# Encoder trunk on one core: the next weight unit split ahead of the sums of one unit, h a step behind its modulation, another order at the beginning

## The chip, the core and the metric

The kernel runs on one core of a Trainium2 chip. The metric is the device time of one execution in microseconds (us). Matrix products run on TensorE (PE, with its weight loads as PEld), elementwise work on VectorE (DVE) and ScalarE (ACT), a few powers on GpSimd (POOL); SyncE (SP) issues the transfers (DMA) from main memory. Each engine works through its own queue in the order in which the program was laid out, and waits at semaphores for what another engine or a transfer has to deliver first.

## What is computed

Two layers (DEPTH 2) over 256 tokens of width 2048, all in float32. What matters here:

```python
c_act = jax.nn.silu(c)
for l in range(DEPTH):
    mod = c_act @ ada_w[l] + ada_b[l]
    sh_a, sc_a, gt_a, sh_m, sc_m, gt_m = [t[:, None, :] for t in jnp.split(mod, 6, axis=-1)]
    h = rmsnorm(x, norm_mix[l]) * (1.0 + sc_a) + sh_a
    qa, ka, va, qb, kb, vb, ga, gb = split_cols(h @ w_in[l])
    ...
    merged = jax.nn.sigmoid(ga) * ya + jax.nn.sigmoid(gb) * yb
    x = x + gt_a * (merged @ w_out[l])
    h = rmsnorm(x, norm_ffn[l]) * (1.0 + sc_m) + sh_m
    u = depthwise_conv(h @ w_up[l], conv_w[l], conv_b[l])
    g, v = jnp.split(u, 2, axis=-1)
    x = x + gt_m * ((jax.nn.silu(g) * v) @ w_down[l])
```

`ya` and `yb` are two kinds of attention over the projected q, k and v. So before the first projection can be complete, x has to be normalised and modulated by `sc_a` and `sh_a`, and these come from a product of silu(c) with a 2048 x 12288 matrix per layer.

## The kernel before

**Weights.** All six weight matrices of a layer are cut into blocks of 128x128 and laid out in the order in which they are used (`block_stream`, L85). Sixteen blocks are a unit of 1 MB. `unit` (L274) fetches one with a transfer on SP into a buffer `raw` (four buffers, shared with the matrix for the modulation), and cuts it into two halves of 8 blocks. Each half is split into a rounded high part, by a cast on ACT (L288), and the rest, by a subtraction on DVE (L289), and both go into a tile `hl` (four buffers, so two units). A product is then three matmuls: high by high, high by low, low by high (L297 to L299 where weights are stationary, L355 to L357 where tokens are). `Stream.next_block` (L318) makes a unit when its first block is wanted, or takes one that was made ahead by `prefetch`.

**Modulation.** `ada` (L203) makes one column block of the modulation at a time: a transfer of 1 MB (aw) and one multiply-and-sum on DVE (L220, called a sum here). 96 per layer. The first 32 of layer 0, in the order shift and scale of chunk 0, of chunk 1, and so on, are needed for h. `normed` (L421) makes one chunk of h (16 chunks of 128 features) from two sums, x and the root mean square: a product on DVE (ht, L427), the high part on ACT (h, L430), the low part on DVE (L431). `ada_and_h` (L616) is the job that runs both: a sum, a sum with its chunk of h, in two steps for each chunk.

**Order at the beginning of layer 0.** There are not yet 16 chunks of h when PE could start, so the input projection is cut along its 2048 input features into three parts, with the ends in `K_ENDS` (L40): 9 groups of 512 columns for q, k and v (`tokens`, L345) and then 16 column blocks for the first gate (`features`, L329), first with the chunks that come early, then with more, then with all; sums of the parts are kept in `packA`, `packB` and `ya` (copied on ACT in the first part, L790 and L827, added on DVE later, L792 and L822). The units of these parts are 0 to 12, 13 to 34 and 35 to 51. Each time a unit's blocks are used up, `Stream.tick` (L314) moves the background jobs by their rates (`Paced`, L234): here `ada_and_h` at `FIRST_RATE` steps per unit; `have_h` (L771) runs that job as far as a group needs. The attention's square roots, transposes (`qk_rows`, L500: norm in one tick, turn in the next) and heads are such jobs too. Afterwards a fixed plan per unit (`ADA_PLAN_0`) sets how many sums there are.

**Before the first matmul.** `cact` holds silu(c), spread over 128 rows by four matmuls and silu on ACT (L168 to L171); squares of x are made in turn on ACT and DVE (L632 to L639), summed over chunks on DVE and over partitions by PE; a power on POOL gives the root. Short matmuls (`warm`, L366) run in between.

The order of the instructions of each engine is laid out when the program is built, by a scheduler that starts from the order of the code; the lists below are what came out of it.

Of the kernel before, what the change touches and what calls it, by code (L numbers as in the profile page):

```python
# [15 lines left out]
P = 128  # L16
# [24 lines left out]
    [([2, 2, 2, 3, 3, 4, 4, 4, 4], 6), ([8, 8, 9, 10, 10, 11, 10, 10, 12], 13), ([KC] * 9, KC)],  # L41
# [20 lines left out]
FIRST_RATE = [1.1, 0.85, 0.7]  # L62
# [67 lines left out]
def encoder(ctx: ExitStack, tc: tile.TileContext, a: dict, out: bass.AP):  # L130
# [37 lines left out]
    for i in range(0, D, 512):  # L168
        cb = ax.tile([P, 512], F32, name="cb", tag="ax")
        nc.tensor.matmul(cb[:], one[:], cact[:1, i : i + 512], start=True, stop=True)  # L170
        nc.scalar.activation(out=cact[:, i : i + 512], in_=cb[:], func=AF.Silu)  # L171
    x = const.tile([P, KC, S], F32, name="x")
    skip(64, const)
# [100 lines left out]
    def unit(l, u):  # L274

        raw = rawp.tile([P, UB * P], F32, name=f"w{l}_{u}", tag="raw")
        nc.sync.dma_start(raw[:], a["ws"][l, u])
        halves = []  # L280
        streamed = any(m == "w_in" and mo < GATE_A // P for m, _, mo in STREAMS[l][u * UB : (u + 1) * UB])
        at = OFF if streamed else 0
        for j in range(2):
            n = UB * P // 2
# [3 lines left out]
            nc.scalar.copy(hl[:, 0], r)  # L288
            nc.vector.tensor_tensor(out=hl[:, 1], in0=r, in1=hl[:, 0].bitcast(F32), op=ALU.subtract)  # L289
# [336 lines left out]
    for i in range(0, KC, 4):  # L626
        nc.sync.dma_start(x[:, i : i + 4], a["xT"][:, i : i + 4])

    mean_sq = sm.tile([P, 2], F32, name="ms_in", tag="nsa")
    with tc.high_priority():  # L630
        acc = place("y0", 4, F32, "sq_in")
        for i in range(0, KC, 4):  # L632
            sq = acc if i == 0 else place(f"y{1 + i // 4 % 2}", 4, F32, f"sq_in{i}")
            if i // 4 % 2:
                nc.vector.tensor_tensor(out=sq[:], in0=x[:, i : i + 4], in1=x[:, i : i + 4], op=ALU.mult)
            else:
                nc.scalar.activation(out=sq[:], in_=x[:, i : i + 4], func=AF.Square)
            if i:
                nc.vector.tensor_tensor(out=acc[:], in0=acc[:], in1=sq[:], op=ALU.add)  # L639
# [35 lines left out]
    for l in range(L):  # L675
        st = Stream(l) if l == 0 else nxt
        mod = mods.get(l)
        if l == 0:
            h = led("h0_0")
            job0 = ada_and_h(first_h(h))  # L680
            while done[0] < 2:
                next(job0)
            st.prefetch(1)
            while done[0] < 2 * K_ENDS[0][0][0][0]:
                next(job0)
            mod = mods[0]
# [84 lines left out]
        def have_h(part):  # L771

            while l == 0 and done[0] < 2 * part.stop:
                next(job0)

        for pi, (groups, gates) in enumerate(parts):
# [3 lines left out]
            for g, part in enumerate(groups):  # L780
# [16 lines left out]
                def have(g=g):  # L797
# [255 lines left out]
```

## Time and profile before

| | us |
|---|---|
| median of 3 runs | 2702.55 (2701.57 to 2703.78) |
| the profiled execution | 2700.72 |
| its span, first to last instruction | 2698.9 |
| PE busy | 2665.7 (99%) |
| PEld busy | 2565.9 (95%) |
| DVE busy | 2089.7 (77%) |
| ACT busy | 1405.0 (52%) |

The views used are the waits (engine, line, what it waited for: us in total, times, the longest), the timeline (start, duration, engine, line, operation, tiles, and in brackets the idle time before it and what ended it), groups of instructions by form (busy time, mean ns of one, idle time before and its cause) and stretches (from:to, length, busy time and instructions of PE, PEld, DVE, ACT and POOL, or of one line alone, then the granted clock, the share of the transfer engines and GB/s). A matmul's bar overlaps the next one, so the pace of PE is read from starts, not from durations. Busy shares over the whole span hide that the beginning is different from the rest: the share of PEld by fortieths of the span begins with 5, 8, 7, 9 tenths.

### The profile page before, as it was taken

Reading aid. Unit: us, or ns where it says so; the run is one execution under the profiler, and the core shown is the slowest. Engines: PE = TensorE matmul, PEld = TensorE weight load, DVE = VectorE, ACT = ScalarE, POOL = GpSimd, SP = SyncE. Lnnn points to the kernel's source line nnn. Section 1 sums busy time; section 2 is a strip of 40 time slices with the busy share of each in tenths; the row PEclk is TensorE's granted clock in tenths of the full one; section 3 lists DMA queues with packets and bytes.
Section 4 is the critical chain, followed back from the end, with each engine's and each line's share of the span. In section 5 each row is a group of like instructions: output and inputs, shape, how many; then the busy total and the mean of one; then the engine's idle time right before and its main releaser. Section 6 shows DMA issues by size and latency. Waiting matters only on the chain.

```text
span 2698.9 us, 50255 instructions
## 1 busy us (share of the span) xinstructions
PE 2665.7 (99%) x21128; PEld 2565.9 (95%) x21128; DVE 2089.7 (77%) x2909; ACT 1405.0 (52%) x2078; POOL 32.6 (1%) x24
## 2 busy tenths in 40 slices
PE   8999999999999999999999999999999999999999
PEld 5879799999999999999998889999999999999999
DVE  8897888897987888788886666658878866655664
ACT  4434685445753455355564556555565445543553
POOL 0000100000000000000000000000000000000000
PEclk9999999999999999999999999999999999999999
DMA  8986678987677788788756656667847775555554
GB/s 348 351 337 242 228 271 327 354 302 265 235 298 292 284 303 285 291 298 289 297 210 255 240 203 239 226 245 253 295 176 283 296 259 193 189 202 188 191 199 141
DMA packets 101892, 700.38 MB, mean 260 GB/s; under 512 B 12705, under 2 KB 15009, under 8 KB 17697
## 3 DMA queue, kind: packets, MB, share of 16 engines
q1 hardware_dynamic: 101666, 697.17, 69.9%
q8 instruction: 165, 2.70, 0.4%
q14 instruction: 61, 0.50, 0.1%
HBM read 695.03 MB, written 2.10 MB: 258 GB/s over the span
## 4 chain that ended last, share of the span: by engine, by line
PE 86%; DVE 8%; ACT 2%; DMA 2%; issue 2%; POOL 1%; SPq 0%; DVEq 0%; ACTq 0%; POOLq 0%
PE ps L297 25%; PE ps L299 25%; PE ps L298 25%; PE ps_t L356 3%; PE ps_t L357 3%; PE ps_t L355 3%; DVE hl L289 3%; DVE aw L220 2%; DMA aw<-in_aw 1%; ACT hl L288 1%; PE po L583 1%; PE sc L552 1%; POOL qrs L402 1%; PE tp L577 0%; DVE qn L516 0%
## 5 line engine op out<-in xcount | busy, mean ns | idle before, releaser
L289 DVE TENSOR_TENSOR hl<-w,hl 128x1024 fp32r<-128x1024 f32 x928 | 1130.0, 1222 | 376.0 <-ACT hl L288 374.8
L288 ACT CAST hl<-w 128x1024 fp32r<-128x1024 f32 x928 | 969.6, 1049 | 732.8 <-PE ps L299 493.9
L297 PE MATMUL ps<-h,hl 128*128 128x256 f32 x3328 | 923.6, 278 | 3.1 <-ACT hl L288 3.1
L299 PE MATMUL ps<-h,hl 128*128 128x256 f32 x3328 | 919.5, 277 | 1.3 <-DVE hl L289 1.3
L298 PE MATMUL ps<-h,hl 128*128 128x256 f32 x3328 | 920.6, 277 | 0.0
L297 PEld LDWEIGHTS ps<-h,hl 128*128 128x128 f32 x3328 | 625.6, 188 | 4.5 <-ACT hl L288 4.1
L299 PEld LDWEIGHTS ps<-h,hl 128*128 128x128 f32 x3328 | 624.8, 188 | 1.8 <-DVE hl L289 1.7
L298 PEld LDWEIGHTS ps<-h,hl 128*128 128x128 f32 x3328 | 625.5, 188 | 0.3
L220 DVE CUSTOM_DVE_ANT_0 aw<-aw,cact,ab 128x2048 f32<-128x2048 f32 x189 | 443.6, 2348 | 55.1 <-DMA aw<-in_aw 54.4
L355 PE MATMUL ps_t<-hl,h 128*128 128x512 f32 x576 | 226.0, 399 | 9.2 <-ACT h L430 4.6
L356 PE MATMUL ps_t<-hl,h 128*128 128x512 f32 x576 | 228.2, 396 | 3.8 <-DVE hl L289 3.3
L357 PE MATMUL ps_t<-hl,h 128*128 128x512 f32 x576 | 226.6, 394 | 0.0
L898 DVE SCALAR_TENSOR_TENSOR u<-ps,cw,u 128x255 f32<-128x255 f32 x304 | 146.2, 481 | 65.4 <-ACT u L896 61.1
L896 ACT ACTIVATE u<-ps,cw 128x256 f32<-128x256 f32 x152 | 85.6, 563 | 182.8 <-PE ps L299 182.6
L299 PE MATMUL ps<-merged,hl 128*128 128x256 f32 x512 | 141.6, 277 | 0.8 <-DVE hl L289 0.8
L298 PE MATMUL ps<-merged,hl 128*128 128x256 f32 x512 | 141.5, 276 | 0.0
L297 PE MATMUL ps<-merged,hl 128*128 128x256 f32 x512 | 141.5, 277 | 0.0
L298 PE MATMUL ps<-act_o,hl 128*128 128x256 f32 x512 | 141.4, 276 | 0.0
L299 PE MATMUL ps<-act_o,hl 128*128 128x256 f32 x512 | 141.3, 276 | 0.0
L297 PE MATMUL ps<-act_o,hl 128*128 128x256 f32 x512 | 141.2, 276 | 0.0
L355 PEld LDWEIGHTS ps_t<-hl,h 128*128 128x128 f32 x576 | 108.6, 189 | 34.2 <-ACT hl L288 6.9
L356 PEld LDWEIGHTS ps_t<-hl,h 128*128 128x128 f32 x576 | 109.2, 190 | 30.9 <-DVE hl L289 8.4
(213 smaller groups left out, 4562.2 us busy)
## 6 DMA issues: line engine op xcount, KB each, us to landing
w<-in_ws SPq DMA_DIRECT2D x464, 1024.0 KB, 4.9
aw<-in_aw SPq DMA_DIRECT2D x189, 1024.0 KB, 6.1
bias<-in_bias SPq DMA_DIRECT2D x16, 256.0 KB, 4.8
x<-in_xT SPq DMA_DIRECT2D x4, 512.0 KB, 5.4
aw_o<-in_aw SPq DMA_DIRECT2D x2, 1024.0 KB, 13.3
out<-x SPq DMA_DIRECT2D x16, 128.0 KB, 2.4
aw_b<-in_aw SPq DMA_DIRECT2D x1, 1024.0 KB, 15.1
cw<-in_cw SPq DMA_DIRECT2D x2, 176.0 KB, 6.0
```

The lines of the kernel that those rows point to most:

```text
L220: nc.vector.tensor_tensor_reduce(out=raw[:], in0=raw[:], in1=cact[:], scale=1.0, scalar=ab[:, i : i + 1], op0=ALU.mult, op1=ALU.add, accum ...
L288: nc.scalar.copy(hl[:, 0], r)
L289: nc.vector.tensor_tensor(out=hl[:, 1], in0=r, in1=hl[:, 0].bitcast(F32), op=ALU.subtract)
L297: nc.tensor.matmul(out, hi, act[0], start=first, stop=False)
L298: nc.tensor.matmul(ps[:, :S], hi, act[1], start=False, stop=False)
L299: nc.tensor.matmul(out, lo, act[0], start=False, stop=last)
L355: nc.tensor.matmul(ps[:], xh, hi, start=kc == kcs[0], stop=False)
L356: nc.tensor.matmul(ps[:], xh, lo, start=False, stop=False)
L357: nc.tensor.matmul(ps[:], xl, hi, start=False, stop=kc == kcs[-1])
L402: nc.gpsimd.tensor_tensor(out=dst, in0=src, in1=mhalf[:, :k], op=ALU.pow)
L896: nc.scalar.activation(out=u, in_=ps, func=AF.Identity, scale=w[:, 1:2], bias=w[:, 3:4])
L898: nc.vector.scalar_tensor_tensor(out=u[:, to], in0=ps[:, of], scalar=w[:, j : j + 1], in1=u[:, to], op0=ALU.mult, op1=ALU.add)
```

## The change

Four things change. (1) While layer 0's units up to 52 are used, each unit's successor is made (transfer, cast, split) as soon as its own first block is taken, so ahead of the sums and chunks of h that the tick at its end brings. (2) The job that runs sums and chunks of h takes three steps for a chunk instead of two: a sum, a sum, the chunk of h; what is done is counted in chunks of h (`have`). The rates and the ends of the second part are set anew; the second part now has units 13 to 33. (3) The very first unit comes in two transfers of half a unit, the first of them made as soon as one chunk of h is there, the second after the second chunk. (4) At the beginning silu(c) goes through other PSUM buffers (`mm`) and stands between the squares in a fixed order, three of the four squares of x are on ACT, and one tiny silu and one tiny power run before any data has come.

```diff
-    [([2, 2, 2, 3, 3, 4, 4, 4, 4], 6), ([8, 8, 9, 10, 10, 11, 10, 10, 12], 13), ([KC] * 9, KC)],
+    [([2, 2, 2, 3, 3, 4, 4, 4, 4], 6), ([7, 7, 9, 9, 9, 10, 10, 11, 12], 13), ([KC] * 9, KC)],
...
-FIRST_RATE = [1.1, 0.85, 0.7]
+FIRST_RATE = [1.2, 1.0, 1.0]
+
+LEAD = 52
...
+    early = const.tile([P, 8], F32, name="early")
+    nc.vector.memset(early[:], 1.0)
+    nc.scalar.activation(out=early[:, 4:5], in_=early[:, 6:7], func=AF.Silu)
+    nc.gpsimd.tensor_tensor(out=early[:, :2], in0=early[:, :2], in1=mhalf[:, :2], op=ALU.pow)
...
-    def unit(l, u):
+    def unit_steps(l, u, by_halves=False):
...
-        nc.sync.dma_start(raw[:], a["ws"][l, u])
+        if not by_halves:
+            nc.sync.dma_start(raw[:], a["ws"][l, u])
...
             r = raw[:, j * n : (j + 1) * n]
+            if by_halves:
+                nc.sync.dma_start(r, a["ws"][l, u][:, j * n : (j + 1) * n])
             nc.scalar.copy(hl[:, 0], r)
             nc.vector.tensor_tensor(out=hl[:, 1], in0=r, in1=hl[:, 0].bitcast(F32), op=ALU.subtract)
             halves.append(hl)
+            if j == 0:
+                yield halves
...
                 self.u, self.at = self.u + 1, 0
+                if self.l == 0 and self.u < LEAD:
+                    self.prefetch(1)
...
         for kc in range(KC):
-            while done[0] < 2 * kc + 1:
+            while done[0] < 2 * kc + 2:
                 next(adas)
                 yield
-            next(adas)
             next(steps)
+            have[0] = kc + 1
             yield
...
+        sqs = []
+        for i in range(KC // 4):
+            sq = place(("y0", "y1", "y2", "a")[i], 12 if i == 3 else 4, F32, f"sq_in{i}")
+            xs = x[:, 4 * i : 4 * i + 4]
+            if i == 1:
+                nc.vector.tensor_tensor(out=sq[:, :4], in0=xs, in1=xs, op=ALU.mult)
+                activated(0)
+                activated(1)
             else:
-                nc.scalar.activation(out=sq[:], in_=x[:, i : i + 4], func=AF.Square)
-            if i:
-                nc.vector.tensor_tensor(out=acc[:], in0=acc[:], in1=sq[:], op=ALU.add)
+                tc.keep_in_program_order(nc.scalar.activation(out=sq[:, :4], in_=xs, func=AF.Square))
+            sqs.append(sq)
+        activated(2)
+        activated(3)
...
-            while done[0] < 2:
+            while have[0] < 1:
                 next(job0)
-            st.prefetch(1)
-            while done[0] < 2 * K_ENDS[0][0][0][0]:
+
+            half = unit_steps(0, 0, True)
+            st.ahead.append(next(half))
+            while have[0] < K_ENDS[0][0][0][0]:
                 next(job0)
+            for _ in half:
+                pass
```

`activated(i)` is the silu of quarter i of c; `have_h` now asks for `have[0] < part.stop`.

What this makes of the queues, at three places. First DVE from the first chunk of h to the first split of unit 1, before (`hl_0_1` is the low part of the second half of unit 0; `aw_o` and `aw_b` are sums 2, 3 and 4; `ht` and `h_0` belong to a chunk of h):

```order
L289 TENSOR_TENSOR hl_0_0_201<-w_0_199,hl_0_0_201 128x1024
L289 TENSOR_TENSOR hl_0_1_204<-w_0_199,hl_0_1_204 128x1024
L220 ISA aw_o,mod_168<-aw_o,cact,ab_169 128x2048
L220 ISA mod_168 128x1
L220 ISA aw_o,mod_168<-aw_o,cact,ab_169 128x2048
L220 ISA mod_168 128x1
L227 SCALAR_TENSOR_TENSOR amod_173<-mod_168,nrm_171 128x1
L427 SCALAR_TENSOR_TENSOR ht<-x,amod_173,rbs 128x256
L220 ISA aw_b_251,mod_168<-aw_b_251,cact,ab_169 128x2048
L220 ISA mod_168 128x1
L431 SCALAR_TENSOR_TENSOR h_0_167<-ht,mod_168,h_0_167 128x256
L289 TENSOR_TENSOR hl_1_0_260<-w_1_258,hl_1_0_260 128x1024
```

The same place on DVE now:

```order
L297 TENSOR_TENSOR hl_0_0_204<-w_0_203,hl_0_0_204 128x1024
L449 SCALAR_TENSOR_TENSOR h_0_171<-ht,mod_172,h_0_171 128x256
L225 ISA aw_o,mod_172<-aw_o,cact,ab_173 128x2048
L225 ISA mod_172 128x1
L225 ISA aw_o,mod_172<-aw_o,cact,ab_173 128x2048
L225 ISA mod_172 128x1
L232 SCALAR_TENSOR_TENSOR amod_177<-mod_172,nrm_175 128x1
L445 SCALAR_TENSOR_TENSOR ht<-x,amod_177,rbs 128x256
L297 TENSOR_TENSOR hl_0_1_218<-w_0_203,hl_0_1_218 128x1024
L449 SCALAR_TENSOR_TENSOR h_0_171<-ht,mod_172,h_0_171 128x256
L297 TENSOR_TENSOR hl_1_0_230<-w_1_228,hl_1_0_230 128x1024
L297 TENSOR_TENSOR hl_1_1_233<-w_1_228,hl_1_1_233 128x1024
```

The split of the second half of unit 0 has moved behind sums 2 and 3, and sum 4 behind unit 1.

Second DVE in the gates of the first part, from chunk 7 of h to the split of unit 10, before:

```order
L427 SCALAR_TENSOR_TENSOR ht<-x,amod_173,rbs 128x256
L431 SCALAR_TENSOR_TENSOR h_0_167<-ht,mod_168,h_0_167 128x256
L289 TENSOR_TENSOR hl_9_0_653<-w_9_651,hl_9_0_653 128x1024
L289 TENSOR_TENSOR hl_9_1_656<-w_9_651,hl_9_1_656 128x1024
L220 ISA aw_14_711,mod_168<-aw_14_711,cact,ab_169 128x2048
L220 ISA mod_168 128x1
L220 ISA aw_15_714,mod_168<-aw_15_714,cact,ab_169 128x2048
L220 ISA mod_168 128x1
L227 SCALAR_TENSOR_TENSOR amod_173<-mod_168,nrm_171 128x1
L427 SCALAR_TENSOR_TENSOR ht<-x,amod_173,rbs 128x256
L431 SCALAR_TENSOR_TENSOR h_0_167<-ht,mod_168,h_0_167 128x256
L289 TENSOR_TENSOR hl_10_0_726<-w_10_724,hl_10_0_726 128x1024
```

The same place on DVE now, from unit 9 to sum 14:

```order
L297 TENSOR_TENSOR hl_9_0_596<-w_9_594,hl_9_0_596 128x1024
L297 TENSOR_TENSOR hl_9_1_599<-w_9_594,hl_9_1_599 128x1024
L225 ISA aw_13_656,mod_172<-aw_13_656,cact,ab_173 128x2048
L225 ISA mod_172 128x1
L232 SCALAR_TENSOR_TENSOR amod_177<-mod_172,nrm_175 128x1
L445 SCALAR_TENSOR_TENSOR ht<-x,amod_177,rbs 128x256
L449 SCALAR_TENSOR_TENSOR h_0_171<-ht,mod_172,h_0_171 128x256
L297 TENSOR_TENSOR hl_10_0_662<-w_10_660,hl_10_0_662 128x1024
L297 TENSOR_TENSOR hl_10_1_665<-w_10_660,hl_10_1_665 128x1024
L297 TENSOR_TENSOR hl_11_0_728<-w_11_726,hl_11_0_728 128x1024
L297 TENSOR_TENSOR hl_11_1_731<-w_11_726,hl_11_1_731 128x1024
L225 ISA aw_14_786,mod_172<-aw_14_786,cact,ab_173 128x2048
```

Sums 14 and 15 stood ahead of unit 10, and stand behind unit 11 now; sum 13 with its chunk has moved from ahead of unit 9 to behind it.

Third PE in the third part, at the transposes `qtp` of the first group of queries, before (`ps_39` and `ps_41` are the sums of the next two groups):

```order
L357 MATMUL ps_39_t_2134<-hl_40_1_2186,h_0_167 128x512
L355 MATMUL ps_41_t_2219<-hl_40_1_2186,h_0_167 128x512
L356 MATMUL ps_41_t_2219<-hl_40_1_2186,h_0_167 128x512
L357 MATMUL ps_41_t_2219<-hl_40_1_2186,h_0_167 128x512
L355 MATMUL ps_41_t_2220<-hl_40_1_2186,h_0_167 128x512
L356 MATMUL ps_41_t_2220<-hl_40_1_2186,h_0_167 128x512
L357 MATMUL ps_41_t_2220<-hl_40_1_2186,h_0_167 128x512
L355 MATMUL ps_41_t_2219<-hl_41_0_2255,h_0_167 128x512
L356 MATMUL ps_41_t_2219<-hl_41_0_2255,h_0_167 128x512
L357 MATMUL ps_41_t_2219<-hl_41_0_2255,h_0_167 128x512
L540 MATMUL qtp<-ident,qn 128x128 x8
```

On PE now, the last of the matmuls between `ps_39` and the transposes:

```order
L375 MATMUL ps_41_t_2233<-hl_40_0_2161,h_0_171 128x512
...
L373 MATMUL ps_41_t_2232<-hl_40_1_2164,h_0_171 128x512
L374 MATMUL ps_41_t_2232<-hl_40_1_2164,h_0_171 128x512
L375 MATMUL ps_41_t_2232<-hl_40_1_2164,h_0_171 128x512
L373 MATMUL ps_41_t_2233<-hl_40_1_2164,h_0_171 128x512
L374 MATMUL ps_41_t_2233<-hl_40_1_2164,h_0_171 128x512
L558 MATMUL qtp<-ident,qn 128x128 x8
```

Between the end of `ps_39` and the transposes stood 9 matmuls, and 17 now.

More of the change, by code (lines that the diff above doesn't have):

```diff
@@ L167, in encoder @@
     nc.vector.memset(one[:], 1.0)
[L168 to L171, printed above, removed]
     x = const.tile([P, KC, S], F32, name="x")
-    skip(64, const)
+    for i in range(0, KC, 4):
+        nc.sync.dma_start(x[:, i : i + 4], a["xT"][:, i : i + 4])
+    skip(32, const)
     skip(224)
@@ L290, in unit @@
             halves.append(hl)
+            if j == 0:
+                yield halves
+    def unit(l, u):
+        steps = unit_steps(l, u)
+        halves = next(steps)
+        for _ in steps:
+            pass
         return halves
@@ L614, in need, with activated @@
             next(adas)
+    have = [0]
     def ada_and_h(steps):
         for kc in range(KC):
-            while done[0] < 2 * kc + 1:
+            while done[0] < 2 * kc + 2:
                 next(adas)
                 yield
-            next(adas)
             next(steps)
+            have[0] = kc + 1
             yield
-    for i in range(0, KC, 4):
-        nc.sync.dma_start(x[:, i : i + 4], a["xT"][:, i : i + 4])
     mean_sq = sm.tile([P, 2], F32, name="ms_in", tag="nsa")
     with tc.high_priority():
[L631 to L635, printed above, removed]
-            else:
-                nc.scalar.activation(out=sq[:], in_=x[:, i : i + 4], func=AF.Square)
-            if i:
-                nc.vector.tensor_tensor(out=acc[:], in0=acc[:], in1=sq[:], op=ALU.add)
+        cbs = []
+        for i in range(0, D, 512):
+            cbs.append(mm.tile([P, 512], F32, name="cb", tag="mm"))
+            nc.tensor.matmul(cbs[-1][:], one[:], cact[:1, i : i + 512], start=True, stop=True)
+        def activated(i):
+            tc.keep_in_program_order(
+                nc.scalar.activation(out=cact[:, 512 * i : 512 * (i + 1)], in_=cbs[i][:], func=AF.Silu)
+            )
+        sqs = []
[6 more added lines that the diff above has]
+                activated(1)
+            else:
+                tc.keep_in_program_order(nc.scalar.activation(out=sq[:, :4], in_=xs, func=AF.Square))
+            sqs.append(sq)
+        activated(2)
+        activated(3)
+        acc = sqs[0]
+        for sq in sqs[1:]:
+            nc.vector.tensor_tensor(out=acc[:], in0=acc[:], in1=sq[:, :4], op=ALU.add)
         for n in (2, 1):
@@ L771, in have_h @@
         def have_h(part):
-            while l == 0 and done[0] < 2 * part.stop:
+            while l == 0 and have[0] < part.stop:
                 next(job0)
@@ L795, in encoder, with turned @@
                     continue
-                def have(g=g):
+                def turned(g=g):
                     ready[0] = g + 1
@@ L804, in encoder @@
                 if g == 0:
-                    qk_rows(pss, GA, rots[1], gains[:, 1:2], kTa, have)
+                    qk_rows(pss, GA, rots[1], gains[:, 1:2], kTa, turned)
                 elif g < 3:
-                    qk_rows(pss, 4, rots[0], gains[:, 0:1], dst, have)
+                    qk_rows(pss, 4, rots[0], gains[:, 0:1], dst, turned)
                 elif vcol is None:
-                    qk_rows(pss, 4, None, gains[:, 3:4] if g in (3, 6) else gains[:, 2:3], dst, have)
+                    qk_rows(pss, 4, None, gains[:, 3:4] if g in (3, 6) else gains[:, 2:3], dst, turned)
                 else:
-                    have()
+                    turned()
                 if g == 2:
```

1 line of the change is left out of this document (added).

## The prediction, made before the changed kernel had run

> **What bounds the kernel now.** Read first the waits of PE, then the stretches, then the timeline. PE is the engine that runs out last: from 1800 to 2400 us it is busy without a break. So only stretches in which PE waits, or runs slowly, can be shortened, and the list of PE's waits up to 206 us shows where they are:
>
> ```profile
> 1800.00:2400.00 600.00, 600.00 (x5233) 599.21 (x5233) 459.90 (x640) 316.01 (x469) 0.70 (x1) 1.00 0.66 239
> PE ps_t L355 <- ACT h L430: 4.6, 1, 4.6
> PE ps_t L355 <- ACT hl L288: 4.6, 6, 1.9
> PE ps_t L356 <- DVE hl L289: 3.3, 4, 1.5
> PE ps L297 <- ACT hl L288: 3.1, 3, 2.6
> PE qtp L540 <- DVE qn L533: 3.9, 2, 2.5
> ```
>
> All are waits for a weight half (hl) or a chunk of h, apart from the last row, which is from the list over the whole span. How much is lost in all is counted in units. A half unit is 8 blocks of 128x128, and there are four hl tiles, so the cast of half n+4 starts when PE has finished half n. The timeline of ACT and a count of casts:
>
> ```profile
> 206.42 1.05 ACT L288 CAST hl<-w 128x1024 fp32r<-128x1024 f32 x1 [1.44 <-PE ps L299]
> 209.14 1.05 ACT L288 CAST hl<-w 128x1024 fp32r<-128x1024 f32 x1 [1.67 <-PE ps L299]
> 0.00:206.40 206.40, 61.43 (x61) 0.98 0.90 344
> ```
>
> PE at its full pace takes 209.14-206.42 = 2.72 us for a half, 5.44 for a unit. The 62nd cast starts at 206.42, so 58 halves were done: 58 x 2.72 = 157.8, and 206.4-157.8 = **48.6 us are lost by then**. From there casts follow every 2.72 us. The same count at two marks on PE:
>
> ```profile
> 21.37 0.73 PE L355 MATMUL ps_t<-hl,h 128*128 128x512 f32 x2 [1.85 <-ACT hl L288]
> 71.53 0.28 PE L297 MATMUL ps<-h,hl 128*128 128x256 f32 x1
> 110.68 0.63 PE L355 MATMUL ps_t<-hl,h 128*128 128x512 f32 x2
> ```
>
> The gates begin at 71.53 after units 0 to 6 (38.1 us of work: 33.4 lost, 21.4 of it before the first matmul); the second K part begins at 110.68 after unit 12 (70.7: 40.0 lost). So the gates lose 6.5 and the second part 8.6.
>
> What feeds PE is DVE, which is in order and has little to spare (DVE, 0 to 206 us, by form):
>
> ```profile
> L289 DVE TENSOR_TENSOR hl<-w,hl 128x1024 fp32r<-128x1024 f32 x61 | 72.3, 1220 | 7.7 <-ACT hl L288 7.6
> L220 DVE CUSTOM_DVE_ANT_0 aw<-aw,cact,ab 128x2048 f32<-128x2048 f32 x29 | 67.9, 2347 | 0.7 <-DMA aw<-in_aw 0.6
> L431 DVE SCALAR_TENSOR_TENSOR h<-ht,mod,h 128x256 fp32r<-128x256 f32 x16 | 7.7, 482 | 5.1 <-ACT h L430 5.1
> DVE hl L289 <- ACT hl L288: 7.6, 13, 1.4
> ```
>
> Its main waits are for ACT, 12.7 us (13 of them, the longest 1.4, for casts; last row, from the waits), and hardly for transfers, 0.6: which work stands next in the queues decides, not the bandwidth.
>
> **The start.** DVE and ACT before the first matmul, and the second chunk of h:
>
> ```profile
> 6.36 1.28 ACT L171 ACT_TABLE_LOAD   x1
> 9.71 1.23 DVE L639 TENSOR_TENSOR sq_in<-sq_in,sq_in 128x1024 f32<-128x1024 f32 x1 [0.58 <-ACT sq_in L637]
> 10.85 1.22 DVE L635 TENSOR_TENSOR sq_in<-x 128x1024 f32<-128x1024 f32 x1
> 14.43 2.35 DVE L220 CUSTOM_DVE_ANT_0 aw<-aw,cact,ab 128x2048 f32<-128x2048 f32 x1
> 16.70 2.35 DVE L220 CUSTOM_DVE_ANT_0 aw<-aw,cact,ab 128x2048 f32<-128x2048 f32 x1
> 19.36 0.48 DVE L427 SCALAR_TENSOR_TENSOR ht<-x,amod,rbs 128x256 f32<-128x256 f32 x1
> 23.63 2.35 DVE L220 CUSTOM_DVE_ANT_0 aw_o<-aw_o,cact,ab 128x2048 f32<-128x2048 f32 x1
> 28.49 0.48 DVE L427 SCALAR_TENSOR_TENSOR ht<-x,amod,rbs 128x256 f32<-128x256 f32 x1
> 29.57 0.80 PE L355 MATMUL ps_t<-hl,h 128*128 128x512 f32 x1 [4.61 <-ACT h L430]
> DMA to landing us min/median/max: 12.7/13.3/13.9
> L219 SPq DMA_DIRECT2D aw_o<-in_aw x2: 328/328/328, 6.6 to 7.8; - x2
> ```
>
> Removed: one square on DVE (1.2 us), its wait of 0.58 for ACT, and a second table load on ACT (1.3); added two tiny operations (early) that run while x is on its way. The sums of squares end about 1.9 us earlier, so the first reduction starts at 12.5 instead of 14.43 and ht at 17.4. The first half unit now comes in a transfer of its own and is cast ahead of the first h, so the first matmul needs only h: 17.4 + 0.52 (19.36 to 19.88) + 0.5 = 18.5 instead of 21.37. Transfers land in series here: aw_o at 6.6+12.7 = 19.3 and 7.8+13.9 = 21.7, one MB in 2.45 us; half of w_0 moved behind them lets each land 1.25 us earlier, 18.1 and 20.5. The sums of chunk 1 run from 19.4 to 23.9 (17.4, and the splits of h and of half 0: 0.4 and 1.14 more, with 0.5 of waits), not from 23.63, and its h is ready at 25.3 where the matmul of 29.57 stood: 4.2 us.
>
> From there I follow the three queues row by row in the new order, with pitches of these rows (sum 2.27, split 1.14, cast 0.95 to 1.05, copy 0.5): units 0 and 1 (32 blocks that need only two chunks) end at 34.5, chunk 2 comes at 38.6, chunk 3 at 48.1, and the gates begin at 65.7 if PE keeps its clock. It has two gaps in the new order, 20.2 to 22.9 (half 0.1 lands at 21.8 and is cast) and 23.3 to 25.3. What gaps of this size cost:
>
> ```profile
> 31.02 0.63 PE L356 MATMUL ps_t<-hl,h 128*128 128x512 f32 x1
> 31.44 0.63 PE L355 MATMUL ps_t<-hl,h 128*128 128x512 f32 x1
> 80.00:100.00 20.00, 17.39 (x136) 17.00 (x134) 15.58 (x20) 9.08 (x15) 0.00 (x0) 0.91 0.96 373
> 92.15 0.41 PE L297 MATMUL ps<-h,hl 128*128 128x256 f32 x1 [2.61 <-ACT hl L288]
> 275.34 1.06 PE L540 MATMUL qtp<-ident,qn 128*128 128x128 f32 x8 [2.49 <-DVE qn L533]
> 276.00:280.00 4.00, 4.00 (x14) 3.26 (x13) 4.00 (x4) 1.84 (x4) 0.00 (x0) 0.59 0.28 43
> ```
>
> After gaps of 4.61, 2.61 and 2.49 us matmuls follow at 0.42 us (31.02 to 31.44), about half the pace, and the granted clock falls to 0.91 of 20 us (1.8 lost) and 0.59 of 4 (1.6). I charge 2.3 for the two new gaps. The Trainium skill speaks otherwise: its page "TensorE: Matmul & The Clock Gate", section "HAM oscillation — how this bites in real kernels", gives the rule "no PE-idle gaps >~3.4µs". By it the 2.61 and 2.49 would have been free; this trace disagrees. The gates begin at 68.0 instead of 71.53: **-3.5** (0 if the gaps return elsewhere, -6 without slow clock).
>
> **The split ahead, in the gates.** The gap at 92.15 is one place of the kind that the change attacks:
>
> ```profile
> 90.66 0.51 ACT L430 ACTIVATE h<-ht,mod 128x256 fp32r<-128x256 f32 x1 [0.70 <-DVE ht L427]
> 91.07 1.98 ACT L288 CAST hl<-w 128x1024 fp32r<-128x1024 f32 x2
> ```
>
> The casts of unit 10 stood behind the activation for h, and that behind two sums. In the new order unit 11 is split right behind unit 10, and the two sums and h follow. From hl_8 to h#8 DVE holds 20.2 us for 4 units of PE (21.8): 8 splits, 4 sums, 2 h. It keeps up, with under 1 us to spare for two units, and each second cast (units 8, 10, 12) still stands behind an h on ACT; followed by hand they are ready 0.8 to 0.1 us ahead of PE, and the second halves 0.3 late. Its transfer moves ahead with each split, and past a transfer of the sums on SP:
>
> ```profile
> w<-in_ws SPq DMA_DIRECT2D x464, 1024.0 KB, 4.9
> aw<-in_aw SPq DMA_DIRECT2D x189, 1024.0 KB, 6.1
> ```
>
> An issue waits for a raw buffer, and the four buffers go round in 4 x 2.3 = 9 us or more of DVE, so 6.1 us of transfer stay hidden; if DVE waits longer at a split, the next transfer waits with it. I take 34.3 us for the 32.6 of work where 39.15 were needed (71.53 to 110.68): **-4.8** (bounds -6.5, nothing lost, and -1).
>
> **The second part and the rates.** A chunk of h takes three steps now, not two, and rates go from 1.1, 0.85, 0.7 to 1.2, 1.0, 1.0: per unit 0.40, 0.33, 0.33 chunks instead of 0.55, 0.43, 0.35. K_ENDS gives up four k steps in this part to go with it. Rows for it:
>
> ```profile
> 124.06 4.63 DVE L289 TENSOR_TENSOR hl<-w,hl 128x1024 fp32r<-128x1024 f32 x4
> 130.87 1.28 DVE L792 TENSOR_TENSOR packA<-ps_t,packA 128x512 f32<-128x512 f32 x2
> 199.09 0.48 DVE L431 SCALAR_TENSOR_TENSOR h<-ht,mod,h 128x256 fp32r<-128x256 f32 x1
> ```
>
> Units 14 to 27 hold 12 sums (27.2), 28 splits (31.9), 16 additions (9.6) and six h with tables (7) in the old order, 75.7 us or 5.4 per unit, which is all that PE's 5.44 allow; in the new one 10 sums and five h, 70.2 or 5.0. The loss of 8.6 should fall to about 3: **-5.6** (bounds -8.2 and +2). The last chunk comes later in DVE's order: it now stands behind 187.9 us of work instead of 163.6, from the first sum on. The old trace took 199.5-14.4 = 185 for 163.6, so 21 us of waits; with as many it would come at 12.5+187.9+21 = 221. It is first needed in unit 36, at about 34.8 + 36 x 5.44 = 231 (34.8 being 48.6 less the terms so far). So it costs nothing.
>
> **The third part.** PE waited 2.49 us at 275.34 for qn, and 1.6 went with the slow clock behind it. The transposes now stand 17 matmuls behind the group that DVE adds between, where 9 stood: from the end of the group before, DVE's rows sum to 12.8 us and PE reaches them after 13.4. That would save 4.1; other transposes move as well, with as little spare: **-3** (bounds -5 and +3).
>
> Sum: -3.5-4.8-5.6-3 = -16.9. The profiled execution took 2700.72 us (its span 2698.9), so 2683.8; the median of the runs shown is 1.8 above it, and I forecast 2685.5.
>
> **Rivals.** (1) The queues change places, and the gain stays at the start: DVE has under 1 us spare per two units, so if each split waits 1.4 us for its cast, as the longest wait listed, the sums behind it come late and PE waits for h instead. What speaks for it is ACT, which waits for PE to free the buffer before it can cast ahead; against it, DVE's small load. Only -3.5 or less remains: 2699, within 0.2% of before (5.4 us, about what a measurement of this kernel can tell from no change). (2) The kernel is slower: the last chunks of h are starved. Splits for the next unit stand ahead of the sums and wait for PE's buffers, so all of DVE's waits fall on the sums. The last chunk has 10 us of slack over 21 us of waits; past 31, each microsecond is PE's, and past 31+14 the start's gains are gone. At 1.5 us for each of 36 units, 54, it is 9 us over that: 2712. Against it: of PE's waits in the old trace only one was for an h. (3) The clock is not lowered, since the two gaps fall differently, and the third part gives all: 2.3 and 2 more, 2681. The rule of the page "TensorE: Matmul & The Clock Gate" of the Trainium skill leads here, too. (4) Half of it: the start and the gates as forecast, the second part as before, the third with as many waits: 2694.
>
> **How the numbers follow.** Forecast 52%, (3) 20%, (4) 14%, (1) 10%, (2) 4%. The range reaches from 2677 (all four lower bounds, -25.7) to 2698, between (4) and (1). Faster by over 0.2%: 85%; within: 11%; slower: 4%.
>
> **What would show it.** The first matmul at 18.5; the gates at 68 and the second part at 102 on PE; no gap near 2.6 us in the gates; casts 2.72 us apart from about unit 29 on, with the 62nd near 192. A granted clock of 1.0 throughout the first 40 us would show the 2.3 wrong. What makes it wrong: waits of DVE on casts beyond 21 us up to the last h, or PE waiting for ACT h rather than for hl.

## The result, and the profile after

The changed kernel takes **2687.61 us** (median of 4 runs, 2687.03 to 2689.52) against 2702.95 (4 runs, 2701.57 to 2703.78) for the kernel before on the same chip: ratio 0.9945, 95% interval 0.9928 to 0.9962, or 15.3 us less. Forecast were 2685.5, with 2677 to 2698 as range. The same kernel once more, in other rounds, gave 0.9952 (0.9938 to 0.9965).

The profiled execution took 2687.88 us, its span is 2686.1. The timeline of PE at five marks: the first matmul, the gates of the first part, the second part, the third part, and the second gate (`gb`). The second gate stands behind the third part's own gates and the product with `w_proj_a`. Below, for the kernel before, are the two marks not yet shown, the third part and the second gate:

```profile
18.94 0.73 PE L373 MATMUL ps_t<-hl,h 128*128 128x512 f32 x2 [0.47 <-ACT h L448]
70.99 0.28 PE L313 MATMUL ps<-h,hl 128*128 128x256 f32 x1
105.54 0.40 PE L373 MATMUL ps_t<-hl,h 128*128 128x512 f32 x1
221.30 0.40 PE L373 MATMUL ps_t<-hl,h 128*128 128x512 f32 x1
415.19 0.28 PE L313 MATMUL ps<-h,hl 128*128 128x256 f32 x1
```

```profile
238.86 0.40 PE L355 MATMUL ps_t<-hl,h 128*128 128x512 f32 x1
429.43 0.28 PE L297 MATMUL ps<-h,hl 128*128 128x256 f32 x1
```

From mark to mark this gives the terms. The changed k ends move 4 k steps of 4 blocks, one unit, from the second part to the third; so 5.44 us are taken from the second part of the old k ends and put to their third.

| stage | before | after | difference | forecast |
|---|---|---|---|---|
| up to the first gate | 71.53 | 70.99 | -0.5 | -3.5 |
| gates of the first part | 39.15 | 34.55 | -4.6 | -4.8 |
| second part with its gates | 128.18 - 5.44 = 122.74 | 115.76 | -7.0 | -5.6 |
| third part, its gates and the product with `w_proj_a` | 190.57 + 5.44 = 196.01 | 193.89 | -2.1 | -3 |
| the rest of the span | 2269.5 | 2270.9 | +1.4 | 0 |

So the start gave almost nothing, and the sizes of the three others came about as forecast. PE's waits up to 206 us, in the list of waits of the changed kernel (sum us, count, longest), and DVE by form over the same stretch:

```profile
PE ps_t L373 <- ACT h L448: 3.6, 3, 1.8
PE ps_t L373 <- ACT hl L296: 3.4, 2, 2.5
PE ps_t L374 <- DVE hl L297: 0.8, 1, 0.8
PE ps L313 <- ACT hl L296: 0.2, 1, 0.2
```

```profile
L297 DVE TENSOR_TENSOR hl<-w,hl 128x1024 fp32r<-128x1024 f32 x66 | 78.0, 1221 | 12.4 <-ACT hl L296 11.5 <-PE ps L315 0.9
L225 DVE CUSTOM_DVE_ANT_0 aw<-aw,cact,ab 128x2048 f32<-128x2048 f32 x26 | 60.9, 2347 | 0.0
```

In the gates one wait of 0.2 is left; all others lie ahead of 50 us. By 206 us DVE has done 66 splits and 26 sums where it had done 61 and 29: the weights are ahead, the sums behind, as intended. The 62nd cast and the one behind it, in ACT's timeline:

```profile
193.24 1.05 ACT L296 CAST hl<-w 128x1024 fp32r<-128x1024 f32 x1 [1.77 <-PE ps L315]
196.10 1.05 ACT L296 CAST hl<-w 128x1024 fp32r<-128x1024 f32 x1
```

It starts at 193.24, 13.2 us earlier than before (forecast "near 192").

### The profile page after: what moved, and what is told of

Its sections match the earlier page's. It is cut to its first block, busy times and chain, and to the rows that moved or that the text cites. A ratio compares the mean times of both kernels' runs of the same rounds, so it can differ in the third digit from the quotient of the medians.

```text
span 2686.1 us, 50251 instructions
## 1 busy us (share of the span) xinstructions
PE 2663.7 (99%) x21128; PEld 2568.6 (96%) x21128; DVE 2086.4 (78%) x2909; ACT 1402.2 (52%) x2077; POOL 33.8 (1%) x25
## 4 chain that ended last, share of the span: by engine, by line
PE 88%; DVE 6%; DMA 3%; issue 2%; ACT 1%; POOL 1%; DVEq 0%; ACTq 0%; POOLq 0%
PE ps L313 24%; PE ps L315 24%; PE ps L314 24%; PE ps_t L374 4%; PE ps_t L375 4%; PE ps_t L373 4%; DMA aw<-in_aw 3%; DVE hl L297 2%; DVE aw L225 1%; PE po L601 1%; PE sc L570 1%; ACT hl L296 1%; POOL qrs L420 1%; PE tp L595 1%; DVE qn L534 0%
```

## Where the start's gain went

PE behind its three gaps of over 1.2 us between the first matmul and 42 us, in the timeline of the changed kernel, then DVE, then ACT from 29 us on (in brackets the idle time ahead of an instruction and what ended it):

```profile
23.46 0.73 PE L373 MATMUL ps_t<-hl,h 128*128 128x512 f32 x2 [2.47 <-ACT hl L296]
25.99 0.79 PE L373 MATMUL ps_t<-hl,h 128*128 128x512 f32 x1 [1.79 <-ACT h L448]
41.98 0.51 PE L373 MATMUL ps_t<-hl,h 128*128 128x512 f32 x1 [1.29 <-ACT h L448]
```

```profile
12.71 2.34 DVE L225 CUSTOM_DVE_ANT_0 aw<-aw,cact,ab 128x2048 f32<-128x2048 f32 x1
29.18 2.34 DVE L225 CUSTOM_DVE_ANT_0 aw_b<-aw_b,cact,ab 128x2048 f32<-128x2048 f32 x1
36.03 2.36 DVE L297 TENSOR_TENSOR hl<-w,hl 128x1024 fp32r<-128x1024 f32 x2 [4.50 <-ACT hl L296]
38.31 2.35 DVE L225 CUSTOM_DVE_ANT_0 aw<-aw,cact,ab 128x2048 f32<-128x2048 f32 x1
40.90 0.49 DVE L445 SCALAR_TENSOR_TENSOR ht<-x,amod,rbs 128x256 f32<-128x256 f32 x1
```

```profile
34.47 0.59 ACT L829 COPY packA<-ps_t 128x512 f32<-128x512 f32 x1 [1.50 <-PE ps_t L375]
34.95 2.00 ACT L296 CAST hl<-w 128x1024 fp32r<-128x1024 f32 x2
41.42 0.51 ACT L448 ACTIVATE h<-ht,mod 128x256 fp32r<-128x256 f32 x1 [3.98 <-DVE ht L445]
```

The first sum starts 1.72 us earlier (12.71, 14.43 before) and the second chunk's matmul 3.6 earlier (25.99, 29.57 before). Then the first of the third chunk's two sums ends at 31.5, and DVE stands still for **4.50 us** ahead of the split of unit 2: its casts stand on ACT behind copies of PE's results (34.47), and these wait for PE. The second sum stands behind that split and starts at 38.31. PE takes up the third chunk at 41.98. (The second profile of the same kernel has the wait too, 3.95 us at 37.90.) The timeline of PE before has it at this place, too:

```profile
41.89 0.50 PE L355 MATMUL ps_t<-hl,h 128*128 128x512 f32 x1 [1.55 <-ACT hl L288]
```

The prediction had the third chunk ("chunk 2" there, counted from 0) at 38.6. Whether this wait is the reason, the second group of experiments asks.

## Experiments: pace and split ahead

The *pace* is how many chunks of h are made in a unit (0.55, 0.43, 0.35 before; 0.40, 0.33, 0.33 after). Each kernel was timed in 5 rounds beside the kernel before; the table with all of them stands after the last.

**No split ahead.** The changed kernel with

```diff
-LEAD = 52
+LEAD = 0
```

> The changed kernel with LEAD = 0: no unit is split ahead of the sums; start, steps, rates and k ends stay. Theory (the terms of the prediction): the gates' 4.8 us come back, and part of the second part's gain with them: 2692.5 to 2698, and PE has a wait of over 2 us for a cast in the gates again. Rival A (the split ahead is worth little; the slower supply of h and the order of steps opened DVE): 2687 to 2689. Rival B (it carries the whole change): 2702 to 2704.

2695.52, ratio 0.9975 (0.9965 to 0.9984). The time is within the theory's range, the place is not: the gates take 35.0 us, with no wait of PE over 0.42 in them, and the second part 116.0, nearly as in the changed kernel (34.55, 115.76). What comes back is the start (gates at 75.10, not 70.99; 55.9 us after the first matmul, where the two profiles of the changed kernel have 52.1 and 51.5) and the third part (196.4, not 193.9).

**The split ahead alone.** The kernel before with

```diff
                 self.u, self.at = self.u + 1, 0
+                if self.l == 0 and self.u < 52:
+                    self.prefetch(1)
```

> The kernel before with the split ahead of units up to 51 alone; old start, old steps, old rates and k ends. Theory (terms add): the gates' 4.8 and the third part's 3 go, 2694 to 2698, and the second part keeps a loss of some 8 us, since DVE's 75.7 us of work for its 14 units stay. Rival A (it carries nearly the whole change): 2687 to 2690. Rival B (without the slower rates the splits ahead and the sums together take more than DVE has, and h comes late): 2700 or more, with PE waiting for ACT h.

2702.82, ratio 1.0001 (0.9991 to 1.0012): nothing gained. The gates take 39.77 us. PE's waits from 70 to 115 us there:

```profile
PE ps L297 <- ACT hl L288: 3.1, 3, 2.7
PE ps_t L358 <- DVE hl L289: 0.5, 1, 0.5
PE ps_t L357 <- ACT hl L288: 0.3, 1, 0.3
```

A wait like the one of 2.61 us that the prediction wanted to remove by the split ahead is still there (2.66), a unit later, again behind two sums and a chunk of h that stand on DVE between the splits of two successive units. Rival B's time came true, though PE waits for casts, not for h as B said.

**The old pace with everything else.**

```diff
-FIRST_RATE = [1.2, 1.0, 1.0]
+FIRST_RATE = [1.65, 1.275, 1.05]
-    [([2, 2, 2, 3, 3, 4, 4, 4, 4], 6), ([7, 7, 9, 9, 9, 10, 10, 11, 12], 13), ([KC] * 9, KC)],
+    [([2, 2, 2, 3, 3, 4, 4, 4, 4], 6), ([8, 8, 9, 10, 10, 11, 10, 10, 12], 13), ([KC] * 9, KC)],
```

> The changed kernel with sums and h as often per unit as before: rates 1.65, 1.275, 1.05 of steps of a third of a chunk (0.55, 0.425, 0.35 chunks a unit), and the old k ends of the second part. Theory (the rates are the second part's term): 5 to 6 us slower than the changed kernel, 2693, the loss being in units 14 to 27. Rival A (with the split ahead the supply of units no longer hangs on the rates): 2687 to 2689. Rival B (DVE too full in the first part): the gates lose too, 2695 or more.

2707.95, ratio 1.0018 (1.0009 to 1.0028): slower than before, by rival B and more. Gates 41.34, second part 125.5.

**The old pace in the first part only** (first rate 1.65, all else as changed).

> The changed kernel with the old pace of chunks in the first part alone (rate 1.65 of steps of a third, 0.55 chunks a unit); second and third part 1.0, k ends as changed. Theory (two sums that fall between the same two splits hold up the casts; the split ahead pays only at about one sum a unit): gates from first to second part take 38 us or more instead of 34.6, the second part keeps its pace, 4 to 6 slower than the changed kernel, 2692 to 2694. Rival A (the pace of the second part with the old k ends made the slow kernel of the last rates slow): within 1.5, 2686 to 2689. Rival B (chunks made early relieve the second part): the gates lose 4, the second part gives 2 or more back, 2689 to 2691.

2697.07, ratio 0.9985 (0.9976 to 0.9994): 9 us over the changed kernel. The gates take 40.66 us, above the theory's 38, and the second part also loses 2.2 (117.96), which no rival had. DVE in the gates of this kernel (73.59 to 114.25) and of the changed one (70.99 to 105.54), by form:

```profile
L225 DVE CUSTOM_DVE_ANT_0 aw<-aw,cact,ab 128x2048 f32<-128x2048 f32 x8 | 18.6, 2347 | 0.0
L297 DVE TENSOR_TENSOR hl<-w,hl 128x1024 fp32r<-128x1024 f32 x14 | 16.4, 1221 | 3.5 <-ACT hl L296 3.5
```

```profile
L297 DVE TENSOR_TENSOR hl<-w,hl 128x1024 fp32r<-128x1024 f32 x13 | 15.2, 1222 | 2.1 <-ACT hl L296 1.1 <-PE ps L315 0.9
L225 DVE CUSTOM_DVE_ANT_0 aw<-aw,cact,ab 128x2048 f32<-128x2048 f32 x6 | 14.0, 2348 | 0.0
```

Eight sums instead of six stand between the splits: 4.6 us more of DVE in a stretch whose work on PE is 32.6. DVE is busy for 35.50 of 40.66 us there, for 30.55 of 34.55 in the changed kernel.

**h in the step of its second sum**, as before, at the changed pace:

```diff
-            while done[0] < 2 * kc + 2:
+            while done[0] < 2 * kc + 1:
                 next(adas)
                 yield
+            next(adas)
             next(steps)
```

(rates 0.8, 0.6667, 0.6667)

> The changed kernel with h made in the step of its second sum, as before: steps of two for a chunk, rates 0.8, 0.667, 0.667, so that a unit still gets 0.40, 0.33, 0.33 chunks; k ends, split ahead and beginning as changed. Theory A (the number of chunks per unit decides, not the step): within 1.5 of the changed kernel, 2687 to 2689. Rival B (a sum and h in one step are 3.6 us of DVE ahead of the next split, and the casts come late): 4 or more slower, 2692 to 2696, with waits of PE for casts in the first and second part.

2690.24, ratio 0.9959 (0.9947 to 0.997): a time between A and B, with an interval that overlaps the changed kernel's. The stages speak for A: gates 35.14, second part 115.76, third 194.3, each within 0.6 of the changed kernel's. That h is made a step later is worth nothing that these runs can tell.

**Split ahead in the first part only** (LEAD = 13).

> The changed kernel with units split ahead up to number 13 only, so in the first part alone. Theory (terms): the gates' 4.8 us are kept (34.3 to 34.6 us from the first gate to the second part), the third part loses its 3 again and the second part little, with DVE's 70 us of work under PE's 76: 2690 to 2692. Rival A (the split ahead is what the second part lives on): the second part loses 3 or more too, 2694 or more. Rival B (only the first part needs it): 2687 to 2688.5.

2694.15, ratio 0.9976 (0.9964 to 0.9988). Gates 34.51, second part 117.99 (+2.2), third part 196.4 (+2.5). The places are the theory's, the time is rival A's: the second part lost more than "little", and 2 us of the difference lie in none of the stages. That it loses more there than the kernel without any split ahead (116.0) is not explained; PE waits 0.36 us at 107.0 and 0.31 at 112.6, at the first units that are not split ahead.

## Experiments: the beginning

**The old beginning in the changed kernel** (squares and silu in the old order, x loaded behind c, no early operations, unit 0 in one transfer).

> The changed kernel with the old beginning: squares and silu in the old order, x loaded behind c as before, no early table and power, unit 0 in one transfer after the first chunk. Theory (the start term as forecast): 3.5 us slower than the changed kernel, 2691. Rival A (as the trace of the changed kernel reads at the mark of the gates, 71.53 before and 70.99 after): at most 0.5 slower, 2688. Rival B (DVE's supply sets the first units, and its first sum comes 1.72 us later): 1.7 slower, 2689.3.

2689.00, ratio 0.9947 (0.9935 to 0.996), not to be told from the changed kernel's 0.9945 and 0.9952. First matmul at 23.22, gates at 73.76; two profiles of the changed kernel have 18.94 and 21.36, and 70.99 and 72.84, so these marks settle nothing below 2 us. The forecast's 3.5 is not to be seen in the time.

**The new beginning alone** (LEAD = 0, old steps, rates and k ends).

> The new beginning alone: squares, silu, early operations, loads and the two transfers of the first unit as changed; LEAD = 0, steps, rates and k ends as before. Theory (the start term as forecast): the gates begin at 68 and the time is 2699, 3.5 under before. Rival A (marks of the runs with and without the new beginning, 71 and 73.8 with all else new): 2.7 under before, gates at 69. Rival B (what PE wins it waits for later, at the next chunk of h): the gates begin at 71 to 72, the time within 1 of before.

2702.50, ratio 1.0004 (0.9996 to 1.0013), gates at 72.59. The time is rival B's. PE's first matmul comes at 18.90, and the row that answers to 41.89 is

```profile
41.74 0.80 PE L373 MATMUL ps_t<-hl,h 128*128 128x512 f32 x1 [3.79 <-ACT hl L296]
```

All that was won is waited for at the third chunk: the wait that the row names is for the cast of unit 2, which stands on ACT behind that chunk's h (40.24 and 40.66). So the start term was wrong by itself, before the split ahead came in.

**The clock.** 20 idle matmuls in PE's first gap:

```diff
+GAPS = [20, 0, 0]
...
+                if self.l == 0 and self.u == 1 and kc == 0:
+                    warm(GAPS[self.at // 8])
```

> The changed kernel with 20 matmuls on the identity, whose result nothing reads, in PE's first gap of 2.47 us (21.0 to 23.5), so that PE stands still for 1.8 us only in what follows. Clock: the half clock of 24.2 to 31.05 goes, and the matmuls of the first two units end 3 us earlier. Time, theory (PE's clock is a term of the start): 2 to 3.4 under the changed kernel, 2684 to 2685.5. Rival (chunks of h set the time to the gates): PE waits 3 us longer for h between 37 and 48, the gates begin at 71 as in the changed kernel, the time 2687 to 2688. If the clock is halved in spite of it, the cause of the slow clock is not that gap.

2690.72 (2686.63 to 2694.2), ratio 0.9961 (0.9948 to 0.9974): the theory's time is not reached. The six runs fall into two groups, 2686.6 to 2688.0 and 2693.5 to 2694.2; the profiled one (2693.47) is of the second. The idle matmuls took 4.4 us (the trace has 40 for 20) and filled both gaps. Granted clock (the eighth column) from 20 to 40 and from 40 to 60 us, in the changed kernel and in this one:

```profile
20.00:40.00 20.00, 15.74 (x56) 11.73 (x56) 15.43 (x16) 8.75 (x12) 0.00 (x0) 0.83 0.85 343
40.00:60.00 20.00, 17.00 (x64) 12.62 (x64) 16.85 (x21) 10.31 (x15) 0.00 (x0) 0.91 0.90 345
```

```profile
20.00:40.00 20.00, 19.05 (x100) 15.33 (x100) 17.10 (x19) 8.67 (x12) 0.00 (x0) 1.00 0.89 358
40.00:60.00 20.00, 17.13 (x65) 13.09 (x66) 17.00 (x19) 10.98 (x16) 0.00 (x0) 0.91 0.92 346
```

The clock is whole again up to 40 us, and 3.4 us of PE are won there; the gates begin at 70.06, 0.9 earlier (1.3 to 1.8 counted from the first matmul), and the time is no better, not even in the faster group. PE's wait ahead of the third chunk grew from 1.29 to 1.97. This speaks for the chunk as what the start lacked, rather than an earlier first matmul or the clock; the next experiment tests it.

**The third chunk ahead of the split of unit 2.** Three steps instead of one after unit 0:

```diff
-            bg.add(job0, FIRST_RATE[0])
+            bg.add(job0, FIRST_RATE[0], 1.81)
```

> The changed kernel with three steps instead of one after unit 0 (the job begins with 1.81 on its account): both sums of the third chunk and its h stand on DVE ahead of the split of unit 2, which waited 4.50 us for its casts there with one of the two sums behind it. Theory (the start's gain was lost in that wait): the third chunk's h is ready by 36 instead of 41.9, PE's gap of 1.29 at 40.7 goes, the gates begin at 68 to 69.5 and the time is 1.5 to 3 under the changed kernel. Rival A (the loss comes back at unit 3, whose cast is behind copies): gates at 70.5 to 71, the time within 1. Rival B (casts of unit 2 now come late): gates after 71.5, slower by 1 or more.

**2683.03** (2681.57 to 2683.36), ratio 0.9933 (0.9921 to 0.9946), and in the same rounds the changed kernel itself:

> The changed kernel itself, unedited, in the same rounds as the two others, to hold them against, and for a second profile of it. Expected: 2687 to 2689; gates at 70.5 to 71.5; the wait of DVE of 4.5 for the casts of unit 2 again; whether the clock is halved at 24 and at 48 again is open, since the windows of the clock begin elsewhere in each execution.

2687.73 (2685.92 to 2689.78), ratio 0.9952 (0.9938 to 0.9965). The two ranges do not meet: 4.7 us less for one number. DVE and the first gate on PE in the timeline of the faster kernel, then its splits on DVE up to 206 us:

```profile
33.81 2.35 DVE L225 CUSTOM_DVE_ANT_0 aw<-aw,cact,ab 128x2048 f32<-128x2048 f32 x1
36.40 0.49 DVE L445 SCALAR_TENSOR_TENSOR ht<-x,amod,rbs 128x256 f32<-128x256 f32 x1
38.70 2.36 DVE L297 TENSOR_TENSOR hl<-w,hl 128x1024 fp32r<-128x1024 f32 x2 [0.45 <-ACT hl L296]
67.91 0.28 PE L313 MATMUL ps<-h,hl 128*128 128x256 f32 x1
```

```profile
L297 DVE TENSOR_TENSOR hl<-w,hl 128x1024 fp32r<-128x1024 f32 x66 | 77.9, 1219 | 5.9 <-ACT hl L296 5.4 <-PE ps L315 0.5
```

The sum that started at 38.31 starts at 33.81, the split behind it waits 0.45 instead of 4.50, and DVE's waits for casts fall from 11.5 to 5.4. The third chunk was ready by 38, not by 36 as expected, but PE no longer waits for it. The gates begin at 67.91 where the changed kernel of the same rounds has 72.84, both with the first matmul at 21.3 to 21.4: 4.9 us, which is the gain in time. The theory holds, with more gained than it said.

**Both together**, 16 idle matmuls:

> The kernel with the third chunk ahead of the split of unit 2 (the fastest so far, 2683.0), and 16 of the idle matmuls on the identity ahead of the first use of half 0.1 on PE, some 3.6 us of the 4.3 in which PE stood still there. PE has no gap over 0.15 us from 28.4 to the gates there, so that half clock (28.35 to 31.77) is PE's own time now. Theory: no half clock before 40, the gates 1.7 earlier after the first matmul (44.9 instead of 46.6), 2681.3. Rival (with PE earlier it waits for the fourth chunk or unit 3 instead): gates 46 to 46.6 after the first matmul, 2682.5 to 2683.5, and a gap over 0.5 between 40 and 52. Other way: the idle matmuls run past the arrival of the second chunk and hold PE up: 2684 or more.

2683.24 (2682.78 to 2685.38), ratio 0.9934 (0.992 to 0.9947). The gates begin at 65.82, 46.3 us after the first matmul at 19.51 (rival; 46.6 without the idle matmuls); the new gap of 0.53 us comes at 36.1, ahead of the stretch in which the rival put it. The clock at the start is worth nothing measurable here either.

The stages of all profiled executions, from the same marks on PE (old k ends set right by 5.44; "third" goes up to the second gate):

| kernel | gates begin | gates | second | third | rest | ratio |
|---|---|---|---|---|---|---|
| before | 71.53 | 39.15 | 122.7 | 196.0 | 2269.5 | 1 |
| changed | 70.99 | 34.55 | 115.8 | 193.9 | 2270.9 | 0.9945 |
| changed, again | 72.84 | 34.64 | 115.8 | 193.8 | 2268.9 | 0.9952 |
| no split ahead | 75.10 | 35.00 | 116.0 | 196.4 | 2274.4 | 0.9975 |
| split ahead to 13 | 71.52 | 34.51 | 118.0 | 196.4 | 2272.2 | 0.9976 |
| split ahead alone | 72.71 | 39.77 | 120.6 | 197.9 | 2271.3 | 1.0001 |
| old pace | 73.37 | 41.34 | 125.5 | 195.8 | 2272.2 | 1.0018 |
| old pace, first part | 73.59 | 40.66 | 118.0 | 193.6 | 2269.4 | 0.9985 |
| h with its sum | 69.52 | 35.14 | 115.8 | 194.3 | 2272.3 | 0.9959 |
| old beginning | 73.76 | 34.53 | 115.8 | 193.7 | 2268.4 | 0.9947 |
| new beginning alone | 72.59 | 38.27 | 122.6 | 195.5 | 2270.6 | 1.0004 |
| idle matmuls | 70.06 | 34.65 | 115.8 | 196.5 | 2274.4 | 0.9961 |
| third chunk first | 67.91 | 34.81 | 115.8 | 194.0 | 2268.8 | 0.9933 |
| both | 65.82 | 34.82 | 115.8 | 194.7 | 2272.4 | 0.9934 |

The rest, the same work in all, scatters by 6 us between single executions; so only the stages ahead of it, and the medians, are compared.

## Why the prediction was right, and where it was not

**The start (-3.5): wrong.** Its first step held in the first profile (first matmul 18.94, forecast 18.5; second chunk 25.99, forecast 25.3); the second profile of the same kernel has 21.36 and 28.40, since the first sum starts 0.65 later there and DVE waits 1.80 us for the root mean square. The step that failed is "From there I follow the three queues row by row": it gave the third chunk at 38.6, while the split of unit 2, ahead of the chunk's second sum on DVE, waited 4.50 us for casts that stand on ACT behind copies waiting for PE. The new beginning alone gained nothing, and moving the chunk's work ahead of that split gained 4.7. The charge of 2.3 for the slow clock was a side issue: PE lost 3.4 up to 40 us (granted clock 0.83; 1.8 in the second profile, 0.91), and keeping the clock up did not shorten the time.

**The gates (-4.8): size and place right, the edit wrong.** They took 34.55 us, forecast 34.3. But the prediction gave this to the split ahead, and it belongs to the pace: 34.5 to 35.1 in every kernel with the changed pace in the first part, without the split ahead as well (35.00), and 38.3 to 41.3 in every kernel with the old one, with it as well (39.77, 40.66, 41.34). The stretch of the gates, before and after:

```profile
71.53:110.68 39.15, 35.71 (x290) 35.12 (x288) 32.96 (x36) 19.48 (x33) 0.00 (x0) 0.96 0.89 342
70.99:105.54 34.55, 34.32 (x289) 33.86 (x288) 30.55 (x33) 18.49 (x32) 0.00 (x0) 1.00 0.95 360
```

Most of the difference of 4.6 us is one place: the wait of 2.61 and the slow clock behind it (0.96 of 39.15, 1.6 us). The timelines of DVE show it in all five kernels with the old pace: once in the gates, two sums and a chunk of h stand between the splits of one unit and of the next, and PE waits 2.6 to 2.8 us behind them. With the changed pace the splits of two units stand in front of such a pair, in the kernel without the split ahead too, and no wait of PE in the gates is over 0.45. The prediction saw this place, and took the split ahead for what would clear it. The load fits as well: DVE is busy for 33.0 us there before, as much as PE's work of 32.6, and for 29.1 in the kernel without the split ahead. That an engine without spare time gains nothing by doing part of its work earlier is thus likely, but no run tells the load from that one place.

**The second part (-5.6): right in cause, low in size.** -7.0, and -6.7 without the split ahead (116.04): the pace, with the k ends that go with it. The split ahead alone gives 2.1 of it. For its 21 units PE needs 21 x 5.44 = 114.2, so 1.5 us are left; they lie in its gates (last section).

**The third part (-3): the size about right, the step wrong.** -2.1. The prediction had PE reach the first transposes after DVE is done with their input (13.4 against 12.8 us), so that the wait for qn goes. It did not go. PE's waits for qn over the whole span of the changed kernel, then the stretch from 260 to 280 us in that kernel and in the one with idle matmuls:

```profile
PE qtp L558 <- DVE qn L551: 4.2, 3, 1.8
260.00:280.00 20.00, 17.36 (x84) 14.38 (x85) 17.41 (x31) 10.36 (x14) 5.19 (x2) 1.00 0.55 205
260.00:280.00 20.00, 19.06 (x86) 15.99 (x87) 17.04 (x29) 10.71 (x14) 5.24 (x2) 0.91 0.56 208
```

Before it was 3.9 us in two waits, now 4.2 in three. The longest fell from 2.49 to 1.81, and the slow clock behind it, 1.6 us before, stayed away. That was luck: behind a wait of 1.94 in the kernel with idle matmuls it is back (0.91), and the third part of that kernel took 196.5, as much as before. The split ahead has its share all the same: in the two kernels that lack it here, PE's waits in this stage sum to 7.8 us instead of 5.2 (5.0 in the second profile), and 2.5 are lost, at a granted clock of 1.00. The split ahead alone, at the old pace, gives nothing there (197.9).

**The sum** thus came out at -12.8 in the profiled executions and -15.3 in the medians (-13.0 when the same kernel was timed again), for 16.9 forecast. So it is near for another reason than the one given: the start's gain is missing, and the gates' and the second part's come from the slower pace. That the terms add is what the prediction took for granted, and it is wrong: split ahead alone 0, slower pace without it (with the new steps and the new beginning) -6.6, new beginning alone 0, all together 13 to 15. So at the changed pace the split ahead is worth 6 to 9 us, and what of it the stages show lies in the start (some 4 us) and the third part (2.5), not in the gates. Together with the old pace the split ahead and the new beginning make the kernel slower (+5.9). The slower pace alone, with nothing else changed, was not run.

**The rivals.** (1), the queues change places and PE waits for h instead: its mechanism is what the start showed, in the one place at 36.03, but not in the gates. (2), starved last chunks: no; the last waits of PE ahead of the third part lie before 50 us, but for 0.2. (3), the clock not lowered: it was, and keeping it up was worth nothing measurable. (4), half of it: no. Of the signs, the first matmul (in one profile of two) and the gates without a gap held, and the casts nearly (the 62nd at 193.24 for "near 192", 2.86 behind it the next, for 2.72); "gates at 68, second part at 102" failed by the start's 3 (70.99, 105.54). Of what would make it wrong, PE waiting for ACT's h is half there: 3.6 us, against 4.4 for hl.

## What to carry to other kernels

Splitting the next operands earlier gave nothing here while the engine that splits was as loaded as the bound one, and 6 to 9 us once the work beside it came at a lower rate: lower that rate first, and look which of the two edits carries the gain. When a start is made earlier, follow the in-order queues up to the next thing that the bound engine needs, and ask of every instruction ahead of it whether it waits for that very engine; here one wait of 4.5 us took back most of the gain, and a reordering by two steps was worth more than the whole new beginning. A term that comes out at its size is not yet right: two of four did so here by another step than the one given. Gains of edits that feed one queue aren't to be added from separate estimates.

## What the runs showed of the chip

- Gaps of 2.47 and 1.79 us on PE, with 0.7 us of matmuls between them, brought the granted clock to 0.83 over 20 us, as the one gap of 4.61 had before: 3.4 us of PE. The Trainium skill's page "TensorE: Matmul & The Clock Gate", section "HAM oscillation — how this bites in real kernels", asks for "no PE-idle gaps >~3.4µs"; here the trace disagrees, since neither of the two gaps was as long. Which gaps do it changes from one execution to the next: in the second profile of the changed kernel 0.29 and 3.98 us at the same place cost half as much (0.91), and at the transposes a gap of 1.94 us was followed by 0.91 over 20 us in one kernel (idle matmuls), one of 2.20 by 1.00 in another (h with its sum).
- The idle matmuls' kernel shows one such drop late: a gap of 2.22 us at 797, and 0.91 from 800 to 820, where the others run at 1.00. So a stage of a single execution can be off by 2 to 3 us here, and the whole by the 6 by which the rest scatters.
- The pitch of matmuls is not always the same at a granted clock of 1.0. In the gates of the second part, 208 to 236 us, with hardly anything beside them but splits, casts and additions, the split ahead alone and the old pace show (PE's count is in the second column):

```profile
208.00:236.00 28.00, 28.00 (x249) 28.00 (x249) 19.85 (x34) 10.96 (x11) 0.00 (x0) 1.00 0.71 247
```

```profile
208.00:236.00 28.00, 28.00 (x240) 28.00 (x240) 18.89 (x33) 10.49 (x10) 0.00 (x0) 1.00 0.67 241
```

  That is 113 against 118 ns from one start to the next, and nearly every one of them is longer. It goes by kernel, not by execution: the kernel before, the split ahead alone and the new beginning alone have 113 in these gates, all others 118, the changed kernel in both of its profiles. Neither a wait nor the DMA share explains it (0.71 with the faster pitch). It makes 1.5 us of the changed kernel's second part; why is open.
